# Layer 2's AdaLN as weighted sums of row tiles on VectorE, in a two-layer transformer trunk on one core

## The chip, the core and the metric

The kernel runs on one core of one Trainium2 chip. The metric is the device time of one execution in microseconds (us). TensorE (PE) multiplies matrices, VectorE (DVE) and ScalarE (ACT) work on tiles in SBUF and PSUM, GpSimd (POOL) on tiles in SBUF, and SyncE (SP) issues the transfers from and to HBM. Every engine works through its own instructions in the order in which the program was scheduled, and waits at an instruction whose inputs or buffers are not ready.

## The reference, cut to what matters

Two layers work on a latent sequence of 1024 tokens and on a context of 256, all with 1024 channels. Each layer's six modulation vectors (AdaLN) come from one product of a silu'd condition with `w_ada[i]`, 1024 rows by 6144 columns; there are two conditions, one for the latent tokens and one for the context:

```
cond = jax.nn.silu(c)
cond_c = jax.nn.silu(c_ctx)
for i in range(DEPTH):
    need_ctx = i < DEPTH - 1
    mod = (cond @ w_ada[i] + b_ada[i])[:, None, :]
    mod_c = cond_c @ w_ada[i] + b_ada[i]
    sh1, sc1, gt1, sh2, sc2, gt2 = jnp.split(mod, 6, axis=-1)
    sh1c, sc1c, gt1c, sh2c, sc2c, gt2c = jnp.split(mod_c, 6, axis=-1)
    a = modulate(h, g_mix[i], sh1, sc1)
    ac = modulate(hc, g_mix[i], sh1c, sc1c)
    ...
    h = h + gt1 * y
    h = h + gt2 * swiglu(modulate(h, g_ffn[i], sh2, sc2), w_gate_up[i], w_down[i])
    if need_ctx:
        hc = hc + gt1c * yc
        hc = hc + gt2c * swiglu(modulate(hc, g_ffn[i], sh2c, sc2c), w_gate_up[i], w_down[i])
return h
```

In the second layer (`i = 1`) the context is only normalised once, with `sh1c` and `sc1c`; its other four vectors are not used.

## The kernel before, in words

Every fp32 product is made of three matmuls on a high and a low part of each operand. `split` (L143, L144) makes the parts: ACT casts the high part, and VectorE or GpSimd subtracts it from the tile to leave the low one. Such pairs lie in pools of 512-column tiles: `wsp` (12 buffers), `pr` (16), and in the back half of a layer `px` (11).

`back(0, o)` is the back half of layer 1. After the output projection and the gate and up products of the latents come two stages on which the change bears.

**Down** multiplies by `w_down` in six groups of the 22 blocks `f` (two blocks, then five times four). A group goes through two column halves `c` and eight output tiles `nt` each; one `nt` takes 6 matmuls in the first group and 12 in the others (L1068, 512 columns), sums into one of four PSUM banks `bm`, and VectorE's `gate` (L848) adds the bank to `px` and so frees it. The blocks' weights and activations are split ahead of it. The loads `rawf<-s_s`, `raw<-w_down` are issued by SP.

**The context's feed-forward** follows: for each of 22 blocks `ctx_gate_up` (48 matmuls of 256 columns, L1129, into a `bm` bank; then L1131 to L1135 for the activation), and after every second block `ctx_down` of the pair before (eight `nt` of 6 matmuls, L1068 with 256 columns, into one of four banks `b`, each freed by a gate of 256 columns). Of every pair's twelve weight tiles GpSimd subtracts eight and VectorE four.

The AdaLN product of layer 2 is cut into three groups of 2048 columns (`ada`, L148). `self.later` holds its generators, and `tick()` takes one step of them after every fifth `nt` of down. A step of `ada(1, i, self.pslot, 2)` loads four tiles of `w_ada` (512 KB each) into `pr` buffers and issues eight matmuls of the condition (32 columns, of which two are used) with them (L161); after four steps `ada_close` copies the bank (L186), transposes it on TensorE (L189) and lets VectorE add the bias and make the gains `gsc`. The order of instructions on each engine is set by a scheduler that runs a timeline of its own; the program's order is the priority.

In the profile `b` is the PSUM tag of `bank()`, and one fp32 matmul leaves two records.

## Time and profile before

| | us |
|---|---|
| median of 3 runs | 2893.75 |
| lowest and highest | 2890.32, 2896.26 |
| the profiled execution's own time | 2896.47 |
| its span (first to last instruction) | 2894.7 |

| engine | busy us | share of the span |
|---|---|---|
| PE | 2812.0 | 97% |
| PEld (weight loads) | 2310.6 | 80% |
| DVE | 1645.7 | 57% |
| ACT | 1119.7 | 39% |
| POOL | 791.0 | 27% |

The busy times are sums over the whole program; the stage of a change has its own shares. Down lies between 1083 and 1357 us of the span, and the context's feed-forward between 1357 and 1560 us.

### The profile page before, as it was taken

The page shows a single profiled execution, that of the slowest core. Times are in us where ns is not written, and L with a number is a line of the kernel's source. Part 1 is how long each engine was busy: PE and PEld are TensorE (multiplying, and loading weights), DVE is VectorE, ACT ScalarE, POOL GpSimd, SP SyncE. Part 2 cuts the span into 40 slices and gives each one's busy share as a digit, 9 for nine tenths or more (in the row PEclk, how much of TensorE's full clock was granted, in tenths as well). Part 3 has the DMA queues.
Part 4 walks back from the last instruction along what each step waited for, and adds up shares of the span by engine and source line. Part 5 has one row for each costly group of instructions (what it writes and reads, how often), then busy time and mean ns, then how long its engine had stood idle before and what let it go on. Part 6 is the DMA issues. An engine that isn't in the chain of part 4 may idle for free.

```text
span 2894.7 us, 42717 instructions
## 1 busy us (share of the span) xinstructions
PE 2812.0 (97%) x15586; PEld 2310.6 (80%) x15586; DVE 1645.7 (57%) x2965; ACT 1119.7 (39%) x2263; POOL 791.0 (27%) x802
## 2 busy tenths in 40 slices
PE   6999999999999999999999999999999999999999
PEld 3667777788888887778999888788788788887887
DVE  5657777658755555446543344166656856556442
ACT  4323666535223232234553222266654423233120
POOL 3443242210121222233873354111101021123220
PEclk8999999999999999999999999999999999999999
DMA  7583342434322248644563464366753422226221
GB/s 269 176 246 97 90 135 81 158 110 133 131 81 84 81 146 301 207 147 134 180 188 111 119 182 117 107 182 162 194 178 125 149 95 77 81 88 207 85 91 62
DMA packets 306178, 404.18 MB, mean 140 GB/s; under 512 B 30128, under 2 KB 165808, under 8 KB 305968
## 3 DMA queue, kind: packets, MB, share of 16 engines
q1 hardware_dynamic: 237072, 362.91, 39.7%
q10 hardware_dynamic: 68896, 38.55, 4.6%
q8 instruction: 123, 2.02, 0.3%
q14 instruction: 87, 0.71, 0.1%
HBM read 317.73 MB, written 83.62 MB: 139 GB/s over the span
## 4 chain that ended last, share of the span: by engine, by line
PE 87%; DMA 4%; DVE 4%; ACT 1%; issue 1%; POOL 1%; SPq 1%; DVEq 0%; ACTq 0%; POOLq 0%
PE b L808 17%; PE bm L1068 16%; PE bm L808 12%; PE bm L354 11%; PE bm L866 7%; PE bm L1129 4%; PE b L602 3%; PE b L354 3%; PE b L590 2%; PE b L1068 2%; DMA qst<-q_s 2%; PE b L730 2%; PE b L746 2%; PE b L557 1%; PE b L161 1%
## 5 line engine op out<-in xcount | busy, mean ns | idle before, releaser
L1068 PE MATMUL bm<-pr,wsp 128*128 128x512 f32 x1920 | 440.3, 390 | 0.0
L1068 PEld LDWEIGHTS bm<-pr,wsp 128*128 128x128 f32 x1920 | 359.2, 188 | 82.1 <-issue 5.9
L808 PE MATMUL b<-wsp,px 128*128 128x512 f32 x1584 | 377.9, 391 | 0.0
L808 PEld LDWEIGHTS b<-wsp,px 128*128 128x128 f32 x1584 | 297.5, 188 | 65.1
L848 DVE SCALAR_TENSOR_TENSOR px<-bm,mod,px 128x512 f32<-128x512 f32 (+1 forms) x232 | 170.7, 739 | 268.6 <-PE bm L1068 220.8
L808 PE MATMUL bm<-pr,px 128*128 128x512 f32 x1296 | 317.1, 392 | 5.2 <-ACT kp L970 5.2
L143 ACT CAST wsp<-raw 128x512 fp32r<-128x512 f32 x306 | 188.3, 620 | 342.5 <-PE bm L1068 116.3
L808 PEld LDWEIGHTS bm<-pr,px 128*128 128x128 f32 x1296 | 243.5, 188 | 59.3 <-ACT kp L970 6.1
L354 PE MATMUL bm<-wsp,pr 128*128 128x512 f32 x1152 | 272.4, 393 | 0.0
L144 POOL TENSOR_TENSOR px<-wt,px 128x512 fp32r<-128x512 f32 x64 | 91.1, 1424 | 628.5 <-ACT px L143 369.9
L354 PEld LDWEIGHTS bm<-wsp,pr 128*128 128x128 f32 x1152 | 213.4, 188 | 43.4
L144 POOL TENSOR_TENSOR wsp<-raw,wsp 128x512 fp32r<-128x512 f32 x132 | 174.7, 1331 | 250.4 <-ACT wsp L143 232.1
L143 ACT CAST px<-wt 128x512 fp32r<-128x512 f32 x176 | 108.3, 621 | 330.5 <-PE b L808 302.4
L144 DVE TENSOR_TENSOR wsp<-raw,wsp 128x512 fp32r<-128x512 f32 x174 | 141.2, 816 | 144.1 <-ACT wsp L143 143.0
L866 PE MATMUL bm<-pr,wsp 128*128 128x512 f32 x768 | 176.8, 390 | 0.0
L354 PE MATMUL b<-wsp,pr 128*128 128x512 f32 x576 | 148.8, 412 | 19.1 <-ACT pr L263 6.6
L866 PEld LDWEIGHTS bm<-pr,wsp 128*128 128x128 f32 x768 | 143.3, 188 | 29.3
L354 PEld LDWEIGHTS b<-wsp,pr 128*128 128x128 f32 x576 | 110.8, 198 | 56.2 <-issue 12.7
L710 DVE CUSTOM_DVE_ANT_0 pr<-b,wsp,big 128x640 f32<-128x640 f32 (+1 forms) x128 | 107.0, 847 | 83.9 <-PE b L705 71.5
L294 POOL TENSOR_TENSOR hrs<-hss,mhalf 128x8 f32<-128x8 f32 (+1 forms) x66 | 104.8, 1587 | 169.2 <-DVE hss L292 164.4
L1166 DVE TENSOR_TENSOR t<-b,kp 128x512 f32<-128x512 f32 x88 | 60.8, 691 | 135.5 <-PE b L808 135.2
L1129 PE MATMUL bm<-prc,wsp 128*128 128x256 f32 x1056 | 134.3, 285 | 0.0
(205 smaller groups left out, 4822.0 us busy)
## 6 DMA issues: line engine op xcount, KB each, us to landing
raw<-w_gu SPq DMA_DIRECT2D x156, 256.0 KB, 2.8
qst<-q_s SPq DMA_DIRECT2D x288, 128.0 KB, 3.1
rawf<-w_gu SPq DMA_DIRECT2D x132, 256.0 KB, 3.1
raw<-w_down SPq DMA_DIRECT2D x110, 256.0 KB, 3.3
wsp<-w_ada SPq DMA_DIRECT2D x48, 512.0 KB, 6.9
pr<-w_ada SPq DMA_DIRECT2D x48, 512.0 KB, 6.5
s_s<-t SPq DMA_DIRECT2D x88, 256.0 KB, 2.0
rawf<-s_s SPq DMA_DIRECT2D x88, 256.0 KB, 3.4
```

Source lines behind the costliest of these rows:

```text
L143: self.nc.scalar.copy(out=w[:, 0, :n], in_=x)
L144: getattr(self.nc, lo).tensor_tensor(out=w[:, 1, :n], in0=x, in1=f32(w[:, 0, :n]), op=ALU.subtract)
L294: nc.gpsimd.tensor_tensor(out=rs[:, :nh], in0=ss[:, :nh], in1=self.mhalf[:, :nh], op=ALU.pow)
L354: self.nc.tensor.matmul(ps, x, y, start=(k == 0 and i == 0), stop=(k == KT - 1 and i == 2))
L602: nc.tensor.matmul(op[64 * r:64 * r + 64, :256], u["v"][:, kts[i], :], u["pt"][i][:, 256 * r:256 * r + 256], start=(i == 0), stop=(i == n ...
L710: nc.vector.tensor_tensor_reduce(out=pt[:, :nl + 256], in0=V, in1=u["bias"][x][m // 7][:, b0:b0 + nl + 256], scale=-1.0, scalar=self.big, ...
L808: self.nc.tensor.matmul(ps, x, y, start=first and k == 0 and i == 0, stop=last and k == 3 and i == 2, skip_group_check=True)
L848: nc.vector.scalar_tensor_tensor(out=h[c, k], in0=ps, scalar=mod[:, ty, k, z:z + 1], in1=h[c, k], op0=ALU.mult, op1=ALU.add)
L866: nc.tensor.matmul(ps[:, :n], x, y, start=(k == 0 and i == 0), stop=(k == KT - 1 and i == 2))
L1068: nc.tensor.matmul(ps, x, y, start=(z == 0 and i == 0), stop=(z == len(parts) - 1 and i == 2))
L1129: nc.tensor.matmul(ps[:, q * CTX:(q + 1) * CTX], x, y, start=(k == 0 and i == 0), stop=(k == KT - 1 and i == 2))
L1166: self.nc.vector.tensor_tensor(out=out, in0=x, in1=y, op=op)
```

## The change

Layer 2's product is made without the condition matmuls. `ada_dve` loads tiles of two row blocks by 512 columns (again 512 KB), and VectorE sums the eight row blocks weighted by the condition's column: one `tensor_scalar` and seven `scalar_tensor_tensor` on 128x512 for each block of 512 columns and each condition. Four matmuls with a column of ones then sum each accumulator over the partitions, which leaves the result with channels on partitions, so that the copy and the transposes go. For the first group (shift and scale) both conditions are summed, for the other two the latent one alone. Groups 0 and 1 take turns, half a column block a step, at the ticks of down; group 2 has its ticks in the context's feed-forward from block 11 on, with tiles in `px` buffers.

```diff
-    def ada(self, layer, grp, slot=None, n=1):
+    def ada(self, layer, grp):
...
+    def ada_dve(self, layer, grp, slot, wt, conds):
+
+        nc, n = self.nc, len(conds)
+        src = self.a["w_ada"][layer, :, grp * 2048:(grp + 1) * 2048].rearrange("(k p) n -> p k n", p=P)
+        for j in range(4):
+            accs = [wt() for _ in conds]
+            for k0 in (0, 4):
+                ts = [slot(F32) for _ in range(2)]
+                for z, t in enumerate(ts):
+                    nc.sync.dma_start(out=t, in_=src[:, k0 + 2 * z:k0 + 2 * z + 2, 512 * j:512 * j + 512])
+                for k in range(k0, k0 + 4):
+                    x = ts[(k - k0) // 2][:, k % 2]
+                    for acc, c in zip(accs, conds):
+                        col = self.cond[:, k, c:c + 1]
+                        if k == 0:
+                            nc.vector.tensor_scalar(out=acc, in0=x, scalar1=col, scalar2=None, op0=ALU.mult)
+                        else:
+                            nc.vector.scalar_tensor_tensor(out=acc, in0=x, scalar=col, in1=acc, op0=ALU.mult, op1=ALU.add)
+                if k0 == 0:
+                    yield
+            ps = self.bank()
+            for z, acc in enumerate(accs):
+                for t in range(4):
+                    b = (4 * z + t) * 2
+                    nc.tensor.matmul(ps[:, b:b + 2], acc[:, t * P:(t + 1) * P], self.ones, start=True, stop=True)
+            ty, kk = grp * 2 + j // 2, slice(j % 2 * 4, j % 2 * 4 + 4)
+            for z, c in enumerate(conds):
+                m = self.mod[layer][:, ty, kk, c]
+                nc.vector.tensor_tensor(out=m, in0=ps[:, 8 * z:8 * z + 8:2], in1=self.bada[:, layer, ty, kk], op=ALU.add)
+                if ty in (1, 4):
+                    g = self.gsc[layer][ty // 3][:, kk, c]
...
+            yield
+
+    def turns(self, *gens):
+        for _ in range(8):
+            for g in gens:
+                next(g)
+                yield
...
-            self.later = [self.ada(1, i, self.pslot, 2) for i in range(3)]
+            self.later = [self.turns(self.ada_dve(1, 0, self.pslot, wt, (0, 1)), self.ada_dve(1, 1, self.pslot, wt, (0,)))]
...
         self.tick(99)
+        self.later = [] if last else [self.ada_dve(1, 2, xslot, wt, (0,))]
...
                 next(mods[1], None)
+                if f > 10:
+                    self.tick()
...
+        self.tick(99)
```

Line numbers above 145 move: the gate is L848 before and L886 after, the down matmuls L1068 and L1106, the adds on gate and up products L1166 and L1208, the context's gate-up matmuls L1129 and L1168, its product with silu L1132 and L1171. New are L181 (`tensor_scalar`), L183 (`scalar_tensor_tensor`), L190 (matmuls with ones) and L194 (bias).

The first place is TensorE in down, its first groups. Before, eight condition matmuls stand after every fifth `nt`:

```order
1398 L161 MATMUL b_10469<-pr,cond 32x512 x8
1399 L1068 MATMUL bm<-pr,wsp 128x512 x39
1400 L161 MATMUL b_10469<-pr,cond 32x512 x8
1401 L1068 MATMUL bm<-pr,wsp 128x512 x60
1402 L189 MATMUL b_10840<-ident,sb 128x128 x4
1403 L1068 MATMUL bm<-pr,wsp 128x512 x60
1404 L161 MATMUL b_10927<-pr,cond 32x512 x8
```

And after the change, at the same place:

```order
1393 L1106 MATMUL bm<-pr 128x512 x64
1394 L190 MATMUL b_10594<-ones,wt 128x2 x4
1395 L1106 MATMUL bm<-pr 128x512 x6
1396 L190 MATMUL b_10594<-ones,wt 128x2 x4
1397 L1106 MATMUL bm<-pr 128x512 x12
1398 L1106 MATMUL bm<-pr,wsp 128x512 x48
1399 L190 MATMUL b_10737<-ones,wt 128x2 x4
1400 L1106 MATMUL bm<-pr,wsp 128x512 x84
```

The condition matmuls and the transposes are gone, and short rows of four matmuls with ones stand between the down matmuls.

The second place is VectorE where down begins; `kp` and `t` are the last sums of the gate and up products (L1166 and L1208), `wsp` and `pr` splits. Before:

```order
1248 L144 TENSOR_TENSOR pr<-rawf,pr 128x512
1249 L1166 TENSOR_TENSOR kp<-b_10321,kp 128x512
1250 L1166 TENSOR_TENSOR kp<-b_10336,kp 128x512
1251 L144 TENSOR_TENSOR wsp<-raw,wsp 128x512
1252 L848 SCALAR_TENSOR_TENSOR px<-bm,mod_89,px 128x512
1253 L1166 TENSOR_TENSOR t<-b_10321,kp 128x512
1254 L1166 TENSOR_TENSOR t<-t,kp 128x512
```

After the change:

```order
1249 L144 TENSOR_TENSOR pr<-rawf,pr 128x512
1250 L181 TENSOR_SCALAR wt<-pr,cond 128x512 x2
1251 L183 SCALAR_TENSOR_TENSOR wt<-pr,cond,wt 128x512 x2
1252 L1208 TENSOR_TENSOR kp<-b_10321,kp 128x512
1253 L183 SCALAR_TENSOR_TENSOR wt<-pr,cond,wt 128x512 x2
1254 L1208 TENSOR_TENSOR kp<-b_10336,kp 128x512
1255 L144 TENSOR_TENSOR wsp<-raw,wsp 128x512
1256 L183 SCALAR_TENSOR_TENSOR wt<-pr,cond,wt 128x512 x2
1257 L886 SCALAR_TENSOR_TENSOR px<-bm,mod_89,px 128x512
1258 L144 TENSOR_TENSOR pr<-rawf,pr 128x512
1259 L886 SCALAR_TENSOR_TENSOR px<-bm,mod_89,px 128x512
1260 L1208 TENSOR_TENSOR t<-b_10321,kp 128x512
```

The first sums stand ahead of the last adds of the gate and up products, and the first gate has eight of them in front of it.

The third place is the end of the first column block of group 2, in the context's feed-forward after block 12. TensorE's rows after the change:

```order
1489 L1106 MATMUL b_13889<-px,wsp 128x256 x6
1490 L1168 MATMUL bm<-prc,wsp 128x256 x122
1491 L190 MATMUL b_13980<-ones,wt 128x2 x4
1492 L1106 MATMUL b_14091<-px,wsp 128x256 x6
1493 L1106 MATMUL b_14099<-px,wsp 128x256 x6
1494 L1106 MATMUL b_14107<-px,wsp 128x256 x6
1495 L1168 MATMUL bm<-prc,wsp 128x256 x3
1496 L1106 MATMUL b_14115<-px,wsp 128x256 x6
```

And VectorE's rows there, between the last gate of one `ctx_down` and the first of the next:

```order
1566 L183 SCALAR_TENSOR_TENSOR wt<-px,cond,wt 128x512
1567 L1171 TENSOR_TENSOR t<-t,bm 128x256
1568 L183 SCALAR_TENSOR_TENSOR wt<-px,cond,wt 128x512
1569 L181 TENSOR_SCALAR wt<-px,cond 128x512
1570 L183 SCALAR_TENSOR_TENSOR wt<-px,cond,wt 128x512 x4
1571 L144 TENSOR_TENSOR wsp<-rawf,wsp 128x512
1572 L194 TENSOR_TENSOR mod_90<-b_13980,bada 128x4
1573 L197 TENSOR_SCALAR gsc_94<-mod_90 128x4
1574 L198 TENSOR_TENSOR gsc_94<-gsc_94,gm 128x4
1575 L886 SCALAR_TENSOR_TENSOR px<-b_14091,mod_89,px 128x256
```

Before, 85 gate-up matmuls stood between two `ctx_down` and none of the rows with `cond`, `ones` or `mod_90`; now 122 stand there, the ones matmuls directly ahead of the next `ctx_down`, and six sums, a split and the bias ahead of its first gate.

## Rows read from the trace of the kernel before

**Rows 1.** The page: the span, and each engine's busy time, share of the span and instructions.

```profile
span 2894.7 us, 42717 instructions
PE 2812.0 (97%) x15586; PEld 2310.6 (80%) x15586; DVE 1645.7 (57%) x2965; ACT 1119.7 (39%) x2263; POOL 791.0 (27%) x802
```

**Rows 2.** The view of stretches: start and end, length, busy time (and instructions) of each engine, granted TensorE clock as a share of full speed, share of the transfer engines, GB/s. First group of down, the rest of down, the way into the context's feed-forward with two pieces of it apart, then the feed-forward.

```profile
1083.00:1107.00 24.00, 24.00 (x121) 17.09 (x119) 13.40 (x18) 6.00 (x10) 7.93 (x6) 1.00 1.01 363
1107.00:1330.00 223.00, 223.00 (x1060) 170.37 (x1057) 105.03 (x160) 55.48 (x100) 56.44 (x45) 1.00 0.56 194
1330.00:1400.00 70.00, 67.84 (x442) 63.08 (x441) 46.97 (x66) 38.87 (x71) 42.10 (x32) 0.95 0.46 149
...
1421.00:1557.00 136.00, 136.00 (x1123) 134.54 (x1122) 65.31 (x120) 66.51 (x127) 96.27 (x77) 1.00 0.56 175
...
1372.00:1384.00 12.00, 12.00 (x90) 12.00 (x89) 4.20 (x8) 6.72 (x14) 9.46 (x9) 0.86 0.46 151
```

**Rows 3.** Everything TensorE waited for between 1083 and 1560 us: who waited for whom, us in total, times, the longest.

```profile
PE b L238 <- DVE acc L230: 2.2, 1, 2.2
```

**Rows 4.** The chain of work that ended last, in order of time: start, us, what (records). Down, and from 1368 us on the context's feed-forward.

```profile
1096.43 1.85 PE b L161 x16
1098.28 7.07 PE bm L1068 x30
...
1128.63 1.85 PE b L161 x16
1130.48 13.87 PE bm L1068 x60
1144.35 0.44 PE b L189 x4
...
1282.71 1.85 PE b L161 x16
...
1341.08 0.79 PE b L238 x8
...
1368.69 1.84 PE b L238 x8
1370.53 8.79 PE bm L1129 x54
...
1455.14 2.74 PE b L1068 x24
...
1461.92 10.18 PE bm L1129 x85
1472.10 2.74 PE b L1068 x24
```

**Rows 5.** All matmul records of L161 that read `pr` tiles: shortest, median and longest in ns, first and last start.

```profile
L161 PE MATMUL b<-pr,cond x192: 592/592/617, 1096.4 to 1284.0; 128*32 128x512 f32 x192
```

**Rows 6.** VectorE's groups over the whole span, shapes kept apart: line, operation, out<-in, count, busy us, mean ns, idle time before.

```profile
L848 DVE SCALAR_TENSOR_TENSOR px<-bm,mod,px 128x512 f32<-128x512 f32 x224 | 166.9, 748 | 267.6 <-PE bm L1068 220.8 <-PE bm L866 44.8 <-DMA px<-h_s 1.8
L900 DVE SCALAR_TENSOR_TENSOR px<-px,mod 128x512 f32<-128x512 f32 x8 | 5.5, 747 | 0.0
L196 DVE TENSOR_TENSOR mod<-b,bada 128x8 f32<-128x8 f32 x24 | 3.7, 156 | 6.6 <-PE b L189 6.6
```

**Rows 7.** Shortest, median and longest ns of L260, which reads two SBUF tiles and a column (as the new sums do) in stretches where GpSimd works too, and of VectorE's splits.

```profile
L260 DVE SCALAR_TENSOR_TENSOR pr<-nt,mod,pr x16: 739/913/1775, 29.9 to 1423.9; 128x512 fp32r<-128x512 f32 x16
...
L144 DVE TENSOR_TENSOR wsp<-raw,wsp x174: 677/692/1782, 24.4 to 2839.8; 128x512 fp32r<-128x512 f32 x174
```

**Rows 8.** The timeline of VectorE, then of GpSimd, in one piece of the context's feed-forward, and VectorE in down: start, us, line, operation.

```profile
1465.63 1.03 DVE L144 TENSOR_TENSOR wsp<-raw,wsp 128x512 fp32r<-128x512 f32 x1 [3.19 <-ACT wsp L143]
...
1464.83 1.29 POOL L144 TENSOR_TENSOR wsp<-raw,wsp 128x512 fp32r<-128x512 f32 x1
1466.08 1.75 POOL L144 TENSOR_TENSOR wsp<-rawf,wsp 128x512 fp32r<-128x512 f32 x1
...
1102.67 0.75 DVE L848 SCALAR_TENSOR_TENSOR px<-bm,mod,px 128x512 f32<-128x512 f32 x1 [0.61 <-PE bm L1068]
1103.34 0.68 DVE L144 TENSOR_TENSOR pr<-rawf,pr 128x512 fp32r<-128x512 f32 x1
```

**Rows 9.** SP's timeline at the first `w_ada` loads, and between 1070 and 1100 us the transfers by kind: count, KB each, median us from issue to landing.

```profile
1075.42 0.42 SPq L155 DMA_DIRECT2D pr<-w_ada  x1
...
1076.95 2.25 SPq L155 DMA_DIRECT2D pr<-w_ada  x3
...
pr<-w_ada SPq DMA_DIRECT2D x8, 512.0 KB, 7.3
px<-hw_s SPq DMA_DIRECT2D x6, 512.0 KB, 7.1
```

**Rows 10.** One pair of blocks of the context's feed-forward (1455.1 to 1472.1 us), by groups: GpSimd, then VectorE.

```profile
L144 POOL TENSOR_TENSOR wsp<-rawf,wsp 128x512 fp32r<-128x512 f32 x4 | 5.6, 1406 | 0.0
L144 POOL TENSOR_TENSOR wsp<-raw,wsp 128x512 fp32r<-128x512 f32 x4 | 5.2, 1291 | 2.2 <-ACT wsp L143 2.2
L1135 POOL TENSOR_TENSOR px<-t,px 128x256 fp32r<-128x256 f32 x2 | 2.2, 1122 | 2.0 <-ACT px L1134 2.0
...
L848 DVE SCALAR_TENSOR_TENSOR px<-b,mod,px 128x256 f32<-128x256 f32 x8 | 3.8, 482 | 2.2 <-PE b L1068 2.1
```

25 lines of the change are left out of this document (12 added, 13 removed).

## The prediction

> **What bounds the kernel now.** I read the page first: TensorE is busy 97% of the span, VectorE 57%, GpSimd 27% [rows 1]. Shares of a whole program say little of two stages, so the view of stretches came next [rows 2]. The reader is to see that TensorE has no gap in down (24.00 of 24 us, 223.00 of 223) nor in the context's feed-forward (136.00 of 136), while VectorE is busy 56%, 47% and 48% there, and GpSimd 33%, 25% and 71%. In the feed-forward the weight loads, too, fill the time (134.54 of 136). The view of waits gives the whole of TensorE's waiting from 1083 to 1560 us: one wait of 2.2 us, at the change from one stage to the other, for an accumulator of VectorE [rows 3]. So time taken from TensorE in these stages is time taken from the kernel, as long as nothing else ends later. The chain [rows 4] agrees: it runs along TensorE's matmuls, and the condition matmuls (L161) stand in it as pieces of their own.
>
> **What leaves TensorE.** 192 records of L161 read `pr` tiles [rows 5], which is 12 rows of 16 records, and each row takes 1.85 us of the chain [rows 4]: 22.2 us. Three rows of transposes at 0.44 us add 1.3. That is 23.5 us. The 592 ns of one record must not be multiplied by 192, since the records overlap.
>
> **What comes to TensorE.** 64 matmuls with ones: 32 for group 0 (two conditions), 16 each for the others, 48 of them in down and 16 in the feed-forward. The same kind stands in the chain as L238, four of them (8 records) in 0.79 us [rows 4]. Sixteen such rows make 12.6 us. TensorE gains 23.5 - 12.6 = 10.9 us, and that is the most this change is likely to give: the ones matmuls cost more than half of what they save, because each loads a full 128-column weight for two columns of work.
>
> **What comes to VectorE.** Group 0 has 4 x 8 x 2 = 64 sums, groups 1 and 2 have 32 each: 96 in down, 32 in the feed-forward. A `scalar_tensor_tensor` of this size takes 0.75 us alone, whether one input is in PSUM (L848) or both are in SBUF (L900) [rows 6], and the next instruction starts 0.67 us after it [rows 8]. I count 0.7. The `tensor_scalar` among them (16 of 128) isn't in the trace at this size; between a 0.16 us instruction on 8 columns [rows 6] and 0.75 I take the same 0.7, which is too much if anything. The small bias and gain instructions cost 0.16 each, as those they replace did.
>
> In the main part of down VectorE is busy 105 of 223 us [rows 2]. About 74 sums (52 us) bring it to 157 of some 210, 75%: there is room. What matters is the longest row of other work between two gates. There are four `bm` banks and 2.77 us of matmuls for each `nt` (60 records, 13.87 us, for five [rows 4]), so a gate may be 3 x 2.77 = 8.3 us late before TensorE lacks a bank. The longest row in the new order has seven sums, two splits and six small instructions, 7 x 0.7 + 2 x 0.69 + 6 x 0.16 = 7.2 us. I count 0 for it, with 4 us as the upper bound, since a split or a sum can take up to 1.78 us when GpSimd works [rows 7].
>
> The beginning of down is tighter. One `nt` of the first group is 6 matmuls, 1.39 us, so the slack there is only 4.2 us. Up to the sixteenth gate the new order has 22 sums, 16 gates, 6 adds and 8 splits, 22 x 0.7 + 16 x 0.7 + 14 x 0.66 = 35.8 us. The first `w_ada` load is issued at 1075.4 and the median to landing was 7.3 us [rows 9], so the sums start near 1082 and, in front of the last gate-and-up adds, hold everything behind them until then. TensorE needs 36 matmuls of gate and up, 96 of down and two rows with ones in that time: 132 x 0.231 + 1.6 = 32 us. VectorE is late by 3.8 us plus waits, less the slack. I take 2 us of stall; the bounds are 0 (half as many `w_ada` tiles are loaded at first, so they may land sooner) and 8 (tiles 4 us later than that).
>
> In the feed-forward the stretch to look at is a pair of blocks, 17.0 us from one `ctx_down` to the next (1455.14 to 1472.10 [rows 4]). VectorE and GpSimd there get into each other's way. The two timelines show it [rows 8]: a split of VectorE that starts at 1465.63 while GpSimd's runs from 1464.83 to 1466.12 takes 1.03 us instead of 0.69 and ends at 1466.66, and GpSimd's next, started at 1466.08, takes 1.75 instead of 1.29. One runs while the other waits, in turn. L260, an instruction like the new sums, shows the same, 0.74 us at best and 1.78 at worst [rows 7]. The budget of a pair: GpSimd's eight splits at 1.25 and two L1135 at about 0.7 (1.12 less the waiting), 11.4 us; VectorE's four splits 2.8; eight new sums 5.6. Together 19.8 us that exclude each other, in a period of 17.0 + 0.8. That is 2 us too much in each of about five pairs. Part is taken up because GpSimd's weights are split ahead: twelve `wsp` buffers are one pair's weights. What isn't taken up reaches TensorE in two ways: the ones matmuls wait for the last sum, and the fourth `nt` of `ctx_down` waits for a `b` bank behind a bias instruction that stands after three or four more sums. I take half, 5 us. The lower bound is 0 (the sums meet GpSimd's idle 4.2 us of each pair [rows 10]), the upper 20 (at each of four column blocks four sums at 1.9 instead of 0.7 us).
>
> The Trainium skill (SBUF — State Buffer, Terms, "shared port pair") says that VectorE and GpSimd arbitrate for one port pair that is held for a full instruction, while the loser blocks. By that rule alone each of the 32 sums could wait 1.25 us, 40 us in all, and the change would lose. The trace agrees that they exclude each other (the pieces of 1.03 and 1.75 us), but at the same time GpSimd's idle time in a pair shows that not every sum will meet it.
>
> **Edits at nothing.** Three copies on ScalarE and the bias adds go; ScalarE is busy 49% in the feed-forward [rows 2], so the gain is nothing. `w_ada` moves as many bytes in tiles of the same size, in rows of 2 KB as `px<-hw_s` has them, which land as fast (7.1 and 7.3 us [rows 9]). 8 MB move to the feed-forward, where the transfer engines are busy 56% [rows 2]; 16 tiles there raise it to some 80%, hidden by the weights' lead, and if the lead is gone each late tile costs what its sum is late, inside the 20 above.
>
> **Sum**, against the profiled execution's 2896.5 us: -23.5 + 12.6 + 2 + 0 + 5 = -3.9, so 2892.6. That execution stood 2.7 us above the median of the three runs, so I forecast 2890.
>
> **The rivals.** *All of it stays hidden.* Then 10.9 us are won, 2883. For it speaks that both engines have room on average, and that TensorE never waited in either stage; against it the order, which puts sums directly ahead of gates and ones matmuls. *The feed-forward goes over.* Each of the four column blocks of group 2 stalls TensorE by 4 us or more, 16 us in all, and the sum is -10.9 + 2 + 16 = +7, 2901; it decides from a stall of about 4 us a block, where 10.9 + 5.8 - 2 = 14.7 us are used up. A stall costs more than itself: after the one wait of 2.2 us the 54 matmuls of 256 columns took 8.79 us, 0.163 each, against 0.120 later (85 in 10.18) [rows 4], and the granted clock was 0.86 in a stretch where TensorE was fully busy [rows 2], so part of it ran at 1.2 instead of 2.4 GHz. That is 2.3 us on 2.2, and 2915 would be four such doubled stalls. *The first tiles land late.* The whole start of down waits behind the first sums, 6 to 8 us instead of 2, and the result is about 2895, no change. That the sums don't replace the matmuls can't be: the order shows L161 gone from down.
>
> **How the numbers follow.** A measurement of this kernel tells 0.2% from no change, 5.8 us: below 2888 is faster, above 2899.5 slower. The forecast, part given back, has 0.45 and lies between 2885 and 2894; 0.17 of it is below 2888. All hidden 0.25, faster. The feed-forward over 0.21, slower. Late tiles 0.09, the same. Faster is 0.25 + 0.17 = 0.42, the same 0.28 + 0.09 = 0.37, slower 0.21. The range of 8 in 10 reaches from 2882 (all hidden) to 2906 (the rival with stalls of some 5 us a block); for the forecast alone it is 2885 to 2894.
>
> **What would show it.** Right: no L161 in down, ones matmuls near 0.79 us a row of four, sums near 0.75 us in down and above 1 us on average in the feed-forward, some waits of TensorE for VectorE's sums (L190) and for banks there. Wrong: no waits at all (then 2883), or waits of more than 4 us at each L190 of the feed-forward, a granted clock below 1 there, or late `w_ada` at the start of down.

## The result and the profile after

The changed kernel takes 2901.27 us in the median of 12 runs (2897.21 to 2906.36), the kernel before 2893.41 in 12 runs beside it (2890.32 to 2899.77). The ratio is 1.0027, with a 95% interval of 1.0019 to 1.0035: slower by about 8 us, where the forecast was 2890, some 4 us faster than the kernel before. The profiled execution of the changed kernel took 2906.36 us; it is the longest of the twelve, 5.1 us above their median, while that of the kernel before stood 3.1 us above its median.

Beside the lines named with the change, L846 are the gate and up products of the latents (L808 before), L276 the statistics matmuls of a norm and L268 the sums they read (L238 and L230 before). First the view of stretches, with the columns of [rows 2]: the first group of down, the rest of it, the way into the context's feed-forward, and the feed-forward. The times are those of [rows 2]; since the changed kernel is some microseconds ahead or behind in them, the work in a row is nearly but not wholly the same.

```profile
1083.00:1107.00 24.00, 18.52 (x72) 13.87 (x71) 23.89 (x31) 6.32 (x11) 8.16 (x6) 0.93 0.88 314
1107.00:1330.00 223.00, 222.68 (x1030) 185.38 (x1029) 157.41 (x238) 54.48 (x97) 60.86 (x44) 1.00 0.48 161
1330.00:1400.00 70.00, 67.84 (x478) 64.60 (x477) 48.18 (x68) 42.11 (x78) 48.28 (x38) 0.95 0.51 164
1421.00:1557.00 136.00, 125.89 (x1007) 124.22 (x1006) 81.65 (x135) 57.10 (x109) 83.60 (x67) 0.96 0.65 217
```

TensorE was busy for all of the first, second and fourth of these stretches; now it lacks 5.5 us at the start of down and 10.1 in the feed-forward, and in both the granted clock is below 1. In the long middle of down it lacks 0.3 us while VectorE is at 157 us. Everything TensorE waited for from 1070 to 1580 us (before: one wait of 2.2 us [rows 3], the fourth row here):

```profile
PE b L190 <- DVE wt L183: 4.8, 3, 2.2
PE bm L1106 <- DVE px L886: 4.4, 3, 3.0
PE b L1106 <- DVE mod L194: 4.1, 2, 2.7
PE b L276 <- DVE acc L268: 2.2, 1, 2.2
PE b L846 <- DVE kp L1208: 1.4, 2, 0.9
PE b L1106 <- DVE px L886: 1.3, 1, 1.3
```

The second and the fifth lie in down, 5.5 of their 5.8 us at its start. The first, third and sixth lie in the feed-forward (10.2 us): TensorE meets the ones matmuls before their sum is ready, and a bank isn't free because VectorE hasn't come to the bias or the gate.

To tell how much each stage lost I use three marks on TensorE's timeline: the first matmul of down, the statistics matmuls of the next norm near the end of down, and the transposes of the context's norm. Of the kernel before, then of the changed one:

```profile
1083.95 1.32 PE L1068 MATMUL bm<-pr 128*128 128x512 f32 x5
1340.91 0.95 PE L238 MATMUL b<-ones,acc 128*128 128x2 f32 x8
1578.44 0.38 PE L249 MATMUL b<-ident,rs 128*128 128x128 f32 x2
```

```profile
1081.94 1.32 PE L1106 MATMUL bm<-pr 128*128 128x512 f32 x5
1332.14 0.95 PE L276 MATMUL b<-ones,acc 128*128 128x2 f32 x8
1590.17 0.38 PE L287 MATMUL b<-ident,rs 128*128 128x128 f32 x2
```

"Down" (first mark to second) went from 256.96 to 250.20 us, 6.8 less. The "feed-forward" (second to third) went from 237.53 to 258.03, **20.5 more**. Outside the marks the program's text is the same, and there the two executions differ by 2.0 us before the first mark and 1.8 us behind the third, so the two profiled executions are 9.9 us apart and the medians 7.9. Below, each kernel is read by these two stretches, of one execution each, as well as by its time.

### The profile page after: what moved, and what is told of

Its sections match the earlier page's. It is cut to its first block, busy times and chain, and to the rows that moved or that the text cites. A ratio compares the mean times of both kernels' runs of the same rounds, so it can differ in the third digit from the quotient of the medians.

```text
span 2904.6 us, 42620 instructions
## 1 busy us (share of the span) xinstructions
PE 2810.9 (97%) x15510; PEld 2326.3 (80%) x15510; DVE 1733.8 (60%) x3089; ACT 1117.3 (38%) x2260; POOL 796.9 (27%) x802
## 4 chain that ended last, share of the span: by engine, by line
PE 83%; DVE 6%; DMA 5%; issue 2%; ACT 1%; POOL 1%; SPq 1%; DVEq 0%; ACTq 0%; POOLq 0%
PE b L846 16%; PE bm L1106 15%; PE bm L846 12%; PE bm L392 11%; PE bm L904 7%; PE b L640 3%; PE b L392 3%; PE bm L1168 3%; PE b L628 2%; PE b L1106 2%; PE b L784 2%; PE b L768 2%; DMA qst<-q_s 2%; PE b L595 1%; PE b L743 1%
## 5 line engine op out<-in xcount | busy, mean ns | idle before, releaser
L1106 PE MATMUL bm<-pr,wsp 128*128 128x512 f32 x1920 | 438.8, 390 | 0.3 <-DVE px L886 0.3
L1106 PEld LDWEIGHTS bm<-pr,wsp 128*128 128x128 f32 x1920 | 359.6, 188 | 74.9 <-ACT pr L143 0.7
L846 PE MATMUL b<-wsp,px 128*128 128x512 f32 x1584 | 378.3, 392 | 1.4 <-DVE kp L1208 1.4
L846 PEld LDWEIGHTS b<-wsp,px 128*128 128x128 f32 x1584 | 297.4, 188 | 67.1 <-DVE kp L1208 2.3
L846 PE MATMUL bm<-pr,px 128*128 128x512 f32 x1296 | 317.0, 392 | 5.2 <-ACT kp L1008 5.2
L886 DVE SCALAR_TENSOR_TENSOR px<-bm,mod,px 128x512 f32<-128x512 f32 (+1 forms) x232 | 169.5, 736 | 208.6 <-PE bm L1106 160.3
L846 PEld LDWEIGHTS bm<-pr,px 128*128 128x128 f32 x1296 | 243.8, 188 | 59.3 <-ACT kp L1008 6.1
L332 POOL TENSOR_TENSOR hrs<-hss,mhalf 128x8 f32<-128x8 f32 (+1 forms) x66 | 104.3, 1580 | 169.1 <-DVE hss L330 164.0
L1208 DVE TENSOR_TENSOR t<-b,kp 128x512 f32<-128x512 f32 x88 | 60.7, 689 | 130.7 <-PE b L846 130.4
L1168 PE MATMUL bm<-prc,wsp 128*128 128x256 f32 x1056 | 135.4, 286 | 0.0
```

The costliest lines, as they stand in the source:

```text
L332: nc.gpsimd.tensor_tensor(out=rs[:, :nh], in0=ss[:, :nh], in1=self.mhalf[:, :nh], op=ALU.pow)
L846: self.nc.tensor.matmul(ps, x, y, start=first and k == 0 and i == 0, stop=last and k == 3 and i == 2, skip_group_check=True)
L886: nc.vector.scalar_tensor_tensor(out=h[c, k], in0=ps, scalar=mod[:, ty, k, z:z + 1], in1=h[c, k], op0=ALU.mult, op1=ALU.add)
L1106: nc.tensor.matmul(ps, x, y, start=(z == 0 and i == 0), stop=(z == len(parts) - 1 and i == 2))
L1168: nc.tensor.matmul(ps[:, q * CTX:(q + 1) * CTX], x, y, start=(k == 0 and i == 0), stop=(k == KT - 1 and i == 2))
L1208: self.nc.vector.tensor_tensor(out=out, in0=x, in1=y, op=op)
```

## The experiments

The four kernels of a first set say where the time is and test the first suspicion; the others followed from what these showed. "Group 2" is the third of layer 2's modulation that the change moved into the feed-forward. All have the changed kernel as their base. The table gives median, ratio to the kernel before with its interval, and what the two stretches gained or lost against before in the trace. The kernel before ran beside each set, with medians of 2892.27 to 2895.14 us, so the ratios are to be compared rather than the medians. Five of the kernels leave out loads or sums and serve only to find the cause: ff_half, ff_noload, ff_unread, ff_psum_noload and ff_ones.

| run | us | ratio, 95% interval | down | feed-forward |
|---|---|---|---|---|
| the changed kernel | 2901.27 | 1.0027, 1.0019 to 1.0035 | -6.8 | +20.5 |
| d01_pe2 | 2890.98 | 0.9994, 0.9984 to 1.0004 | -4.6 | 0.0 |
| pe01_ff2 | 2905.52 | 1.0043, 1.0028 to 1.0057 | -8.9 | +19.4 |
| ff_ahead | 2900.99 | 1.0023, 1.0011 to 1.0034 | -7.6 | +14.3 |
| ff_half | 2896.32 | 1.0005, 0.9994 to 1.0017 | -7.7 | +10.5 |
| ff_noload | 2903.36 | 1.0038, 1.0023 to 1.0052 | -7.3 | +18.0 |
| ff_unread | 2900.57 | 1.0031, 1.0017 to 1.0044 | -7.2 | +17.8 |
| ff_psum | 2905.94 | 1.0037, 1.0025 to 1.0050 | -7.5 | +13.6 |
| ff_lo_dve | 2893.26 | 0.9999, 0.9988 to 1.0011 | -6.4 | +9.6 |
| ff_psum_noload | 2885.84 | 0.9974, 0.9963 to 0.9985 | -6.6 | +5.4 |
| ff_ones | 2887.47 | 0.9977, 0.9965 to 0.9989 | -6.6 | +3.0 |
| ff_ones_late | 2900.20 | 1.0021, 1.0012 to 1.0031 | -7.1 | +19.1 |
| entry_late | 2904.00 | 1.0043, 1.0029 to 1.0056 | -10.1 | +17.7 |
| all_down | 2887.29 | 0.9982, 0.9974 to 0.9991 | -6.0 | +4.7 |
| all_down_psum | 2878.73 | 0.9943, 0.9929 to 0.9957 | -10.2 | +0.1 |

Between entry_late and the changed kernel nothing differs in the feed-forward, and their stretches there differ by 2.8 us; differences of that size say nothing below.

### Where: one stage at a time

```
-    self.later = [] if last else [self.ada_dve(1, 2, xslot, wt, (0,))]
+    self.later = []                       # and one step of pe2 at every 16th block of down
+    pe2 = self.ada_pe(1, 2, self.pslot, 2)     # the old condition matmuls, group 2
```

> Groups 0 and 1 on VectorE in down as in the change, group 2 again by 32 condition matmuls into one bank in down (one pair of its row tiles at every 16th block), so that nothing is added to the context's feed-forward. Theory (the loss lies in the feed-forward, down gained 6.7 us by the two traces): a third of the removed 23.5 us, 7.8, is back in down, so down gains -6.7 + 7.8 = about +1 against before, and the feed-forward gains and loses nothing: 2892 to 2896, ratio 0.9995 to 1.001. Rival (the loss is general, by what the sums do to the DMA queues or to the clock in the whole program): at least half of the 8 us stays, 2897 or more, ratio 1.0013 or more.

And the reverse, the old way in down and VectorE in the feed-forward alone:

```
-    self.later = [self.turns(self.ada_dve(1, 0, ...), self.ada_dve(1, 1, ...))]
+    self.later = [self.ada_pe(1, i, self.pslot, 2) for i in range(2)]
```

> Groups 0 and 1 by condition matmuls in down as before, group 2 on VectorE in the context's feed-forward as in the change. Theory (feed-forward loses about 20 us by itself): -7.8 for the 32 condition matmuls that left down, +20 in the feed-forward: about +12, 2903 to 2908, ratio 1.0035 to 1.005, and the waits of the feed-forward as in the changed kernel. Rival (the feed-forward suffers only since down ended earlier or left the queues in another state): 2893 to 2898.

The times came out by the theory, the first 1 us below its range: 2890.98 and 2905.52 us. In d01_pe2 the feed-forward takes 237.52 us as before, and in pe01_ff2 it loses 19.4 with a down that was done the old way. So the loss belongs to group 2 in the feed-forward alone. For the down of d01_pe2 the expectation was wrong: about 1 us more than before was expected, and it takes 4.6 less. Groups 0 and 1 are on VectorE there as in the change, yet its first group of down has hardly a gap and the full clock:

```profile
1083.00:1107.00 24.00, 23.58 (x104) 16.53 (x104) 22.85 (x33) 5.40 (x9) 5.73 (x4) 1.00 1.00 350
```

TensorE's waits in down are 0.4 us in all. So the stall at the start of down in the changed kernel isn't a fixed price of these sums.

### The first suspicion: tiles that come late

In the changed kernel VectorE's timeline shows long idle times in front of a sum (idle time and what ended it in brackets; the piece behind the first idle time of a pair):

```profile
1459.00 1.03 DVE L144 TENSOR_TENSOR wsp<-rawf,wsp 128x512 fp32r<-128x512 f32 x1 [0.35 <-ACT wsp L143]
1466.66 0.75 DVE L183 SCALAR_TENSOR_TENSOR wt<-px,cond,wt 128x512 f32<-128x512 f32 x1 [6.63 <-DMA px<-w_ada]
1467.33 0.68 DVE L144 TENSOR_TENSOR wsp<-raw,wsp 128x512 fp32r<-128x512 f32 x1
1467.93 0.74 DVE L183 SCALAR_TENSOR_TENSOR wt<-px,cond,wt 128x512 f32<-128x512 f32 x1
1468.59 0.41 DVE L1171 TENSOR_TENSOR t<-t,bm 128x256 f32<-128x256 f32 x1
1468.92 0.74 DVE L183 SCALAR_TENSOR_TENSOR wt<-px,cond,wt 128x512 f32<-128x512 f32 x1
1469.58 0.94 DVE L181 TENSOR_SCALAR wt<-px,cond 128x512 f32<-128x512 f32 x1
1470.45 4.03 DVE L183 SCALAR_TENSOR_TENSOR wt<-px,cond,wt 128x512 f32<-128x512 f32 x4
1474.40 1.77 DVE L144 TENSOR_TENSOR wsp<-rawf,wsp 128x512 fp32r<-128x512 f32 x1
```

VectorE stands 6.63 us before a tile of `w_ada` here, and 23.6 us in five such places of the feed-forward; then come eight sums, of which the last four take 4.03 us (two in a row take 1.40 where nothing holds them up), and a split of 1.77 instead of 0.68. TensorE meanwhile waits 2.17 us for the sum. The transfer it waits for was issued at 1460.62, behind weights of `w_gu` for which SP waited for a buffer. Two causes offer themselves: the late tile, and the slow sums and splits behind it. ff_ahead moves each step's loads one step ahead; ff_half leaves every second sum out:

```
+        if todo:
+            held.append(load(*todo.pop(0)))      # the next step's two tiles
-            ts = [slot(F32) for _ in range(2)] ...
+        ts = held.pop(0)
```

> The changed kernel with the two tiles of each step of group 2 loaded one step (one context column f, about 12 us) before the sums that read them; sums, matmuls and everything else as in the change. Theory A (late loads: w_ada is issued by SP's queue only 6 to 7 us before the sums need it, VectorE stands at the head of its queue): VectorE's 24 us of idle time before w_ada in the feed-forward go, TensorE's 10 us of waits and the 6 us of lower clock mostly go too: 10 to 16 us under the changed kernel, 2885 to 2891, ratio 0.997 to 0.999. Theory B (VectorE and GpSimd wait for each other at their shared way to SBUF; the loads are only what VectorE would have idled for anyway): at most 4 us under the changed kernel, 2897 to 2901, ratio 1.0013 to 1.0027.

```
-                for k in range(k0, k0 + 4):
+                for k in range(k0, k0 + 4, 2 if part else 1):
```

> The changed kernel with only every second row tile of group 2 added up (16 of its 32 sums left out, so layer 2's last modulation is incomplete), all loads, ones matmuls and biases kept and at their places. Theory A (late loads): the tiles come as late as before, and only the sums behind them are shorter, about 2 us in each of 4 column blocks that went over: 3 to 6 us under the changed kernel, 2895 to 2898. Theory B (the sums' own time and their collisions with GpSimd, 25 us of sums at 916 ns): half of the sums take away at least half of the 16 us that lie beyond the ones matmuls, 8 us or more: 2893 or less, ratio 1.000 or less.

Neither settled it. ff_ahead stayed where theory B had it (2900.99), yet its feed-forward is 6.2 us shorter, and VectorE still stood 15.9 us before `w_ada`: the scheduler put the loads into SP's queue in four bunches of four, the second at 1456.08, and the first sum that reads one of that bunch began at 1462.77, so most of the lead was lost. ff_half took 10 us from the stretch, as B says, and came to 2896.32 us, as A says.

### Taking the late tiles away altogether

```
+        if not once or j + k0 == 0:           # only the first pair is loaded
             ts = [slot(F32) for _ in range(2)]
             for z, t in enumerate(ts): nc.sync.dma_start(...)
```

> The changed kernel with only the first two of group 2's sixteen w_ada tiles loaded; all 32 sums, the ones matmuls and the biases stay, and every sum reads those two tiles (layer 2's last modulation is therefore wrong in value). From the end of down to the transposes of layer 2's first context norm took 237.5 us before and 258.0 in the changed kernel (+20.5), 251.9 with the loads a step ahead (+14.3), 248.1 with half of the sums (+10.6). Theory A (VectorE's idle time before the w_ada tiles is what takes it over): that idle time, 24 us, goes; what stays are the ones matmuls (3.8) and a little: +4 to +8, so 2886 to 2891. Theory B (the sums' own time and their collisions with GpSimd): +13 or more, 2896 or more.

ff_unread keeps all sixteen loads, but into tiles that nothing reads:

```
-            ts = [slot(F32) for _ in range(2)]
-            for z, t in enumerate(ts): nc.sync.dma_start(...)
+            us = [slot(F32) for _ in range(2)]
+            for z, t in enumerate(us): nc.sync.dma_start(...)
+            if not once or j + k0 == 0:
+                ts = us
```

> The changed kernel with all sixteen loads of group 2 issued where they stand, but every sum reads the first pair of tiles, so that VectorE waits for no later one (wrong in value as in the run without loads). If it is the wait of VectorE alone that costs: as the run without loads, +4 to +8 us over before in the feed-forward. If the 512 KB transfers themselves delay the weights behind them in the same queue: as the changed kernel or the run with loads a step ahead, +13 to +20.

Theory A fell. With no tile to wait for but the first, ff_noload still loses 18.0 us (2903.36), and ff_unread 17.8 (2900.57). The view of VectorE's groups in the feed-forward shows why; of the changed kernel, and then of ff_noload (L184 are its sums; count, busy us, mean ns, idle time before):

```profile
L183 DVE SCALAR_TENSOR_TENSOR wt<-px,cond,wt 128x512 f32<-128x512 f32 x28 | 25.4, 916 | 18.9 <-DMA px<-w_ada 18.7
```

```profile
L184 DVE SCALAR_TENSOR_TENSOR wt<-px,cond,wt 128x512 f32<-128x512 f32 x28 | 33.4, 1242 | 0.0
...
1421.00:1557.00 136.00, 126.05 (x1015) 123.48 (x1014) 89.70 (x138) 56.27 (x109) 88.12 (x69) 0.97 0.51 164
```

The idle time is gone, and the same 28 sums take 33.4 us instead of 25.4. TensorE is busy 126.05 us of 136, as in the changed kernel. What lengthens the sums is seen in a piece of ff_unread's timeline, VectorE and then GpSimd (L185 are its sums):

```profile
1471.07 6.93 DVE L185 SCALAR_TENSOR_TENSOR wt<-px,cond,wt 128x512 f32<-128x512 f32 x5
```

```profile
1472.37 1.74 POOL L144 TENSOR_TENSOR wsp<-rawf,wsp 128x512 fp32r<-128x512 f32 x1
1474.07 1.71 POOL L144 TENSOR_TENSOR wsp<-raw,wsp 128x512 fp32r<-128x512 f32 x1
1475.74 1.71 POOL L144 TENSOR_TENSOR wsp<-rawf,wsp 128x512 fp32r<-128x512 f32 x1
```

Five sums take 6.93 us instead of some 3.4, and GpSimd's splits beside them 1.7 instead of 1.29 [rows 8]: the two work in turn. My reading is that in the changed kernel VectorE's waits for tiles gave GpSimd time of its own, and that without them the two meet more often.

By its number ff_unread also fits its rival, that the transfers delay the weights. ScalarE does wait longer for `w_gu` tiles where the sixteen loads are made: 15.7 us in the changed kernel and 12.4 in ff_unread from 1421 to 1557 us, 3.9 in ff_noload, 0.4 before. But the longest wait of TensorE in ff_unread, 5.4 us up to 1479.34, comes from the sums shown here: the product with silu stands behind them on VectorE, ScalarE waits 5.6 us for it, and TensorE waits for ScalarE's next cast of a weight. Only one of its waits, 1.1 us, has a late `w_gu` tile behind it in the chain.

### Taking the exclusion away

In all these traces the operations of VectorE with one input in PSUM keep their time. The gates of 256 columns take 478 ns on average in the changed kernel's feed-forward, 479 in ff_noload, and 482 in a pair of before [rows 10]. So the partial sums were put into a PSUM bank (one of the four `bm` that the gate and up products use), and only the last of eight sums writes the SBUF tile:

```
+            sums = [psum() for _ in conds] if psum else accs
-  scalar_tensor_tensor(out=acc, in0=x, scalar=col, in1=acc, ...)
+  scalar_tensor_tensor(out=acc if k == 7 else s, in0=x, scalar=col, in1=s, ...)
```

> The changed kernel with group 2's partial sums held in a PSUM bank: the first seven sums of a column block write and read PSUM, the eighth reads PSUM and writes the SBUF tile that the ones matmuls read. Same sums, loads, matmuls and places. In every trace so far VectorE's operations with a PSUM operand keep their time (gates of 256 columns 478 to 481 ns, with or without sums) while those with SBUF operands alone reach 1.78 us beside GpSimd. Theory B1 (VectorE and GpSimd exclude each other where all of VectorE's operands are in SBUF): sums fall from 916 ns to about 0.75, the splits of both engines stop being held up by them, and the feed-forward falls from +20.5 to +10 or less: 2889 to 2894. Theory B2 (only the time that 32 sums stand in VectorE's in-order queue): 32 x 0.17 = 5 us less on VectorE, of which a part shows: +15 to +20, 2897 to 2901.

The sums now take their plain time; VectorE's groups in the feed-forward of ff_psum:

```profile
L184 DVE SCALAR_TENSOR_TENSOR bm<-px,cond,bm 128x512 f32<-128x512 f32 x24 | 18.0, 750 | 17.0 <-DMA px<-w_ada 16.9
...
L184 DVE SCALAR_TENSOR_TENSOR wt<-px,cond,bm 128x512 f32<-128x512 f32 x4 | 3.0, 739 | 0.0
```

They take 750 ns instead of 916, so the sums that GpSimd held up were those whose inputs were all in SBUF. The Trainium skill (SBUF — State Buffer, Who interferes with whom) says that a VectorE instruction with at most one SBUF input, outside the two-port modes, doesn't contend with GpSimd; the trace agrees. But the feed-forward still loses 13.6 us, between the two expectations: VectorE still stands 16.9 us before the tiles for these sums, and TensorE's added waits, 5.5 us, are all for the last sums of a block.

The time of this run, 2905.94, can't be laid to that stretch. Behind the third mark its execution takes 10.9 us more than the changed kernel's, 1325.3 against 1314.4. TensorE's order is another one in layer 2's attention, long behind the change, and its longest waits between 1900 and 2200 us were, in the changed kernel and in ff_psum:

```profile
PE b L740 <- DMA qst<-q_s: 6.5, 12, 1.7
```

```profile
PE b L741 <- DMA qst<-q_s: 13.9, 16, 2.6
```

That the order makes the difference isn't shown: entry_late has the same one, with 10.7 us of these waits and only 1.2 us more behind the mark, and the kernel before has 11.7 us of them. d01_pe2 and pe01_ff2 have another order that differs in fewer places there; in the other kernels TensorE has the order of the changed one.

The other side of the exclusion is GpSimd. ff_lo_dve takes four of its eight subtractions in each pair away and gives them to VectorE:

```
-  W = [self.unit(a["w_down"][0, ...], "gpsimd", raws=(self.raw, rawf)) ...]
+  W = [self.unit(a["w_down"][0, ...], "vector", raws=(self.raw, rawf)) ...]
```

> The changed kernel with the low halves of the context's w_down tiles (four 128x512 subtractions in each pair of blocks, 1.3 to 1.4 us each on GpSimd) computed on VectorE instead (0.68 us each when nothing holds it up). Theory B1 (exclusion between the two engines): GpSimd is out of the way for some 5.6 us a pair while VectorE gets 2.7 us more, so the feed-forward gets no worse, +12 to +20: 2892 to 2901. Theory B2 (VectorE's queue alone): 2.7 us more a pair on VectorE in a feed-forward that it already holds up, another 5 to 13 us: +25 or more, 2905 or more.

VectorE got 14 us more to do and the kernel was 8 us faster than the changed one (2893.26), its feed-forward 10.9 us shorter:

```profile
1421.00:1557.00 136.00, 131.80 (x1069) 129.61 (x1068) 95.86 (x172) 60.20 (x118) 52.95 (x42) 0.99 0.68 225
```

VectorE's busy time rises from 81.65 to 95.86, GpSimd's falls from 83.60 to 52.95, and TensorE is busy 131.80 us instead of 125.89. The loss of 9.6 us is smaller than either theory had it. So the plain length of VectorE's work (B2) isn't what costs. The run by itself can't tell the exclusion from GpSimd merely having less to do; ff_psum_noload below can, since GpSimd keeps all its subtractions there.

### Both at once, the floor, and TensorE's queue

ff_psum_noload joins the diffs of ff_psum and ff_noload:

```
-        self.later = [] if last else [self.ada_dve(1, 2, xslot, wt, (0,))]
+        self.later = [] if last else [self.ada_dve(1, 2, xslot, wt, (0,), self.bankm, True)]
```

> Partial sums of group 2 in PSUM and, besides, only its first two w_ada tiles loaded (every sum reads those two, so layer 2's last modulation is wrong in value). From the end of down to the transposes of layer 2's first context norm: +20.5 us over before in the changed kernel, +13.6 with PSUM alone, +18.0 without the loads alone. Theory C1 (two causes that each suffice: VectorE is made late either by waiting for the tiles or by exclusion with GpSimd, so that one taken away leaves the other): +4 to +8, little more than the 3.8 us of ones matmuls. Theory C2 (24 us of sums in VectorE's queue and the ones matmuls in TensorE's are the cost, whatever the sums wait for): +12 or more.

ff_ones has ff_noload's loads and the first operation of each column block alone:

```
-                for k in range(k0, k0 + 4):
+                for k in range(k0, 0 if once and k0 else k0 + (1 if once else 4)):
```

> Of group 2 only the first two w_ada tiles are loaded and only the first operation of each column block's sum is made (4 of 32; layer 2's last modulation is wrong in value); the 16 ones matmuls, banks and biases stay. Under every theory but one this is the floor of the feed-forward: 3.8 us of ones matmuls, +3 to +5 over before. If the matmuls, banks and biases themselves hold up TensorE's and VectorE's queues: +8 or more.

ff_ones_late puts what follows a block's sums into `close()` and calls it one block later:

```
+            todo.append(close)                # bank, ones matmuls, bias, scale of block j
+            if len(todo) > late:
+                todo.pop(0)()
```

> The changed kernel with the ones matmuls, the bias and the scale of each column block of group 2 written one column block (two steps, about 21 us) behind its sums; all loads and sums where they were. Theory D (TensorE meets the ones matmuls in its in-order queue before VectorE has the sums, and the bank waits on the bias: 10 us of waits and what the clock loses after them): those waits go, +5 to +11 over before instead of +20.5, 2885 to 2892. Rival (VectorE is late for the splits and gates as well, and TensorE then waits for these instead): +15 or more, 2896 or more.

With both causes away the feed-forward loses 5.4 us (2885.84), and the floor, with two of the loads and four of the sums left, is 3.0. TensorE's waits from 1335 to 1590 us in ff_psum_noload:

```profile
PE b L278 <- DVE acc L270: 2.2, 1, 2.2
PE b L1108 <- DVE px L888: 1.1, 1, 1.1
```

The first stood there before the change. So theory C1 holds. From +20.5, taking away the tiles alone gives +18.0 and the exclusion alone +13.6, but both together +5.4: 2.5 and 6.9 us one by one, 15.1 in one. Each cause suffices to make VectorE late. In ff_ones_late the wait for the ones matmuls is gone, and TensorE's waits are now, beside the 2.2 us that stood there before,

```profile
PE b L1118 <- DVE px L898: 11.6, 6, 3.2
```

for gates: 11.6 us in place of 10.2, a stretch of +19.1, 2900.20 us. Theory D fell. It doesn't matter at which instruction TensorE meets a VectorE that is late.

### The start of down, and another place for group 2

```
-                    if n % 5 == 0:
+                    if n % 5 == 0 and n > 5:
```

> The changed kernel with its first step at the 10th block of down instead of the 5th (sixteen steps, 10 to 85), so that no w_ada tile is asked for while the last products still run. Theory (the entry of down cost 5.8 us of waits and 1.7 of lower clock because VectorE waited for the first w_ada tile and then added up while GpSimd split): these waits go, 5 to 8 us under the changed kernel in down, 2893 to 2897. Rival (VectorE goes over wherever the first sums stand): the same waits some 12 us later, 2899 to 2902.

The 5.8 us of waits in down became 3.2, in four places between 1092 and 1112 us, and down takes 3.4 us less than in the changed kernel. That is less than the 5 to 8 us of the theory; some waits moved with the first sums. The time, 2904.00, is a miss: it lies above both expectations. The trace doesn't show why, since the profiled execution, 2897.50 us, was the fastest of eight that reach to 2911.13.

```
-    self.later = [self.turns(...groups 0 and 1...)]
+    self.later = [self.turns(...groups 0 and 1...), self.ada_dve(1, 2, self.pslot, wt, (0,))]
-                    if n % 5 == 0:
+                    if n % 4 == 0 and n > 4:
```

> All three groups on VectorE in down, none in the context's feed-forward: a step at every fourth block from the eighth on, group 2 after groups 0 and 1. If VectorE has room in down (105 of 223 us before, 157 with groups 0 and 1, about 180 with all three by 27 us of sums): the 23.5 us of condition matmuls and transposes go, 12.6 of ones matmuls come, nothing is lost in the feed-forward: -11, less 0 to 5 of waits: 2883 to 2890, ratio 0.996 to 0.998. Rival (VectorE or the w_ada tiles go over in down as they did in the feed-forward): 2892 or more.

all_down_psum gives `self.bank` to the three, so that their partial sums lie in PSUM as in ff_psum:

> All three groups in down, as in the run that was 0.9982 of before, with the partial sums in PSUM banks. Its down took 250.9 us (before 257.0) with 5.1 us of TensorE waits at the entry, and its feed-forward 242.3 (before 237.5) with one wait of 4.1 us for the last sums. Theory B1: the sums run at about 0.75 us, the two sums of 3.46 us and the split of 1.77 us at the entry fall to their uncontended times, and 3 to 6 us more are gained: 2881 to 2885, ratio 0.996 to 0.997. Theory B2: within 2 us of the run without PSUM, 2885 to 2889.

all_down is 0.9982 of before, at the edge of its expectation: VectorE is busy 173 of 223 us in the main part of down and TensorE still lacks only 0.3 us there, but one wait of 4.1 us for the last sums falls into the way to the feed-forward. With the partial sums in PSUM it is **0.9943** (0.9929 to 0.9957), 2878.73 us, faster than both kernels and more than theory B1 had expected (2881 to 2885). Its stretches, and then all waits of TensorE between 1070 and 1590 us:

```profile
1083.00:1107.00 24.00, 22.11 (x90) 17.73 (x89) 23.85 (x35) 6.83 (x11) 7.87 (x6) 0.93 1.03 367
1107.00:1330.00 223.00, 223.00 (x1047) 186.78 (x1046) 164.02 (x259) 55.89 (x98) 55.00 (x44) 1.00 0.54 181
1421.00:1557.00 136.00, 136.00 (x1085) 132.95 (x1084) 63.10 (x114) 63.95 (x124) 89.52 (x71) 1.00 0.52 169
```

```profile
PE b L191 <- DVE wt L184: 2.0, 1, 2.0
PE bm L1107 <- DVE px L887: 1.9, 1, 1.9
```

3.9 us of waits are left, 164 us of work on VectorE instead of 173 in the main part of down, and a feed-forward as before. The ratio makes it 16.5 us faster than before; the two stretches show 10.1 of them, the rest lies outside the marks, and why isn't shown. What PSUM changes at the start of down is seen in VectorE's first sums; of the changed kernel, then of all_down_psum:

```profile
1080.79 3.00 DVE L181 TENSOR_SCALAR wt<-pr,cond 128x512 f32<-128x512 f32 x2 [4.86 <-DMA pr<-w_ada]
1083.71 1.40 DVE L183 SCALAR_TENSOR_TENSOR wt<-pr,cond,wt 128x512 f32<-128x512 f32 x2
1085.04 0.68 DVE L1208 TENSOR_TENSOR kp<-b,kp 128x512 f32<-128x512 f32 x1
1085.63 3.46 DVE L183 SCALAR_TENSOR_TENSOR wt<-pr,cond,wt 128x512 f32<-128x512 f32 x2
```

```profile
1080.68 1.41 DVE L182 TENSOR_SCALAR b<-pr,cond 128x512 f32<-128x512 f32 x2 [4.38 <-DMA pr<-w_ada]
1082.00 1.40 DVE L184 SCALAR_TENSOR_TENSOR b<-pr,cond,b 128x512 f32<-128x512 f32 x2
1083.31 0.68 DVE L1209 TENSOR_TENSOR kp<-b,kp 128x512 f32<-128x512 f32 x1
1084.08 1.41 DVE L184 SCALAR_TENSOR_TENSOR b<-pr,cond,b 128x512 f32<-128x512 f32 x2
```

These seven operations take 8.3 us in SBUF beside GpSimd (1080.79 to 1089.09) and 4.8 us with PSUM (1080.68 to 1085.49). In all_down, which differs from all_down_psum by the banks alone, they take 8.2 (1079.67 to 1087.85).

## Why the prediction failed, point by point

The forecast had 12.0 us less in down (14.0 saved, 2 of stall) and 8.2 more in the feed-forward (3.2 for ones matmuls, 5 of lateness). The traces show 6.8 less and 20.5 more. The failed step is the feed-forward's lateness.

**What leaves and comes to TensorE in down: right.** L161 is gone from down. 23.5 us less twelve rows of ones matmuls (9.5) is 14.0. The trace shows a gain of 6.8; of the 7.2 between them 5.8 are waits, nearly all at the start of down, and the granted clock of 0.93 over the 24 us there is worth some 1.7, an estimate.

**The entry of down: mis-sized.** 2 us were taken, inside bounds of 0 to 8. It was 5.5 us of waits and the clock. The reckoning gave every sum 0.7 us; the first two took 3.00 us and the fifth and sixth 3.46, beside GpSimd. The exclusion that the forecast saw in the feed-forward was left out here. The first tile wasn't late: the sums began at 1080.79, where 1082 was reckoned. That d01_pe2 has only 0.4 us of waits with the same sums shows that the size depends on how they fall among GpSimd's splits and the gates; what decides that isn't shown.

**The rest of down: right for TensorE, by luck for VectorE.** TensorE lost 0.3 us there, where 0 was taken and 4 was the bound, so the slack of four banks was enough. 157 us were forecast for VectorE and 157.41 came, but the parts cancel: the sums took 64.7 us instead of 52 (896 ns on average over all of down instead of 0.75 us), and VectorE's splits of `pr` and `wsp<-raw` took 30.2 us, where they had taken 39.4 before.

**The feed-forward: the step that failed.** The term was 5 us beside the 3.2 for its ones matmuls, with bounds of 0 and 20; it was 17.5 (20.5 less the floor of 3.0 that ff_ones shows), near the upper bound. Three things in it were wrong. First, the budget of a pair counted only the time that VectorE and GpSimd exclude each other, and put the lateness at "2 us too much" in each of about five pairs (32 sums at eight a pair fill four), of which half would be taken up. Second, the late tiles were costed at nothing in the sum, "hidden by the weights' lead", with only the bound of 20 to cover them. The transfer engines were busy 65%, less than the 80% that was reckoned, but the loads stood in SP's queue behind the weights, and VectorE stood 23.6 us before them with splits and gates queued behind it. These two don't add. ff_noload and ff_psum show that taking one away leaves most of the loss, and ff_psum_noload that taking both away leaves 5.4. As I read it, a budget that adds such terms, and halves them for slack, uses the same idle time of VectorE twice: once to wait for a tile, once to make room for GpSimd. Third, the clock: the forecast added no clock loss to its own term, only to the rival. The granted clock was 0.96 on average in the feed-forward's row, where it had been 1.00, which is an estimated 0.04 x 136 = 5.4 us. With 3.0 for the ones matmuls and 10.2 of waits that makes 18.6 of the 20.5. Right behind the wait of 2.17 us the clock was 0.53, so nearly all of this row at 1.2 instead of 2.4 GHz:

```profile
1472.30:1475.60 3.30, 3.30 (x17) 3.30 (x18) 3.26 (x3) 1.31 (x3) 2.96 (x3) 0.53 0.15 57
```

The chain has this piece as 16 records of `ctx_down` in 3.33 us

```profile
1472.30 3.33 PE b L1106 x16
```

against 24 in 2.74 us before [rows 4], 0.208 us each instead of 0.114.

**The rivals.** "The feed-forward goes over" came true nearly to the number: 16 us of stalls and 2901 us were written, with 0.21. Its mechanism was right as far as it went (late sums ahead of ones matmuls and gates, and a stall that costs more than itself). That the number fits so well is partly luck: the start of down lost 7 us where it had 2, no single wait reached its 4 us a block, and outside the marks the traces gained 3.8 us. Its price for four doubled stalls, 2915, comes to some 2917 by its own terms. "All of it stays hidden" is what all_down_psum does, in another place and with the sums in PSUM: 10.1 us in the two stretches, of 10.9. "The first tiles land late" had the size of the entry about right, but not the cause.

**The signs that were named.** Ones matmuls near 0.79 us a row: yes, 0.79 to 0.80 for each row that stands by itself in the chain in down; in the timeline, which gives such a row 0.95, the four of the feed-forward have 0.98 to 1.05, and three of them follow a wait. Sums near 0.75 us in down: only in the median (742 ns), 896 on average. Sums above 1 us on average in the feed-forward: 916 ns with the idle times in front of the tiles, 1242 without them. A granted clock below 1 there, named as a sign of being wrong: yes, 0.96. Waits at L190 and for banks: yes, 2.2 and 2.7 us at the longest, below the 4 us that were to mark the rival, whose price came from shorter waits in more places and from the clock.

**Left open.** The 1.9 us of the feed-forward's 20.5 that neither waits, clock nor ones matmuls explain are less than the scatter of 2.8 us between two equal feed-forwards. What the delayed `w_gu` tiles cost by themselves wasn't separated: no run has the sums in PSUM and loads that nothing reads. Why the stretch behind the third mark takes between 1310.0 and 1325.3 us in kernels whose text is the same there, and why the order in layer 2's attention is another in four of them, isn't shown.

## What to carry to other kernels

Where a stage has one engine that must not wait, don't look for room on the helping engines by their busy shares: VectorE was busy 48% of this feed-forward, and 28 us of new work cost 20 us. Count what the new work waits for, which engine it holds up and is held up by, and what stands behind it in its queue, and remember that two causes of lateness that each suffice must be removed together before either shows. Sums over many SBUF tiles on VectorE beside a busy GpSimd belong in PSUM, at least the running sum: here that made 0.9943 of the 0.9982 that moving the work to a quieter stage gave alone.

## What the runs showed of the hardware

An fp32 `tensor_scalar` of 128x512 from SBUF to SBUF takes 0.48 us in the median and up to 1.57 beside GpSimd; the same operation into PSUM takes 0.75 us and keeps it (741 to 753 ns in all_down_psum). The Trainium skill (VectorE: DVE Perf Modes, Why PSUM operands drop a tier) says that a PSUM operand caps fp32 at one element a cycle; the trace agrees with it. The slower form belongs to the kernel that was faster here. The shortest, median and longest of the changed kernel's operations in down, and then of the first operation in all_down_psum:

```profile
L183 DVE SCALAR_TENSOR_TENSOR wt<-pr,cond,wt x84: 732/742/1789, 1083.7 to 1259.1; 128x512 f32<-128x512 f32 x84
...
L181 DVE TENSOR_SCALAR wt<-pr,cond x12: 471/478/1569, 1080.8 to 1231.6; 128x512 f32<-128x512 f32 x12
...
L182 DVE TENSOR_SCALAR b<-pr,cond x16: 741/745/753, 1080.7 to 1361.7; 128x512 f32<-128x512 f32 x16
```

Removing the wait for the tiles in the feed-forward made the sums there 326 ns slower each (916 to 1242 ns on average), so an engine's waits can hide what it would lose to its neighbour. And an edit in one stage changed TensorE's order in another, 300 us later or more, in four of the kernels: a kernel whose order is planned as a whole has to be compared stage by stage, not by its time alone.
